# First norm of each layer: scales and biases in the first group's forget-gate buffers, and the scaled centring in two halves

## The chip, the cores and the metric

The kernel runs on one core of one Trainium2 chip. The metric is the device time of one execution in microseconds (us). Timed runs are separate from the profiled execution, which has a time of its own. The engines are PE (TensorE, matrix products), DVE (VectorE), ACT (ScalarE), POOL (GpSimd) and SP (SyncE, which here issues all transfers). Each engine works through its own list of instructions in order, so an instruction that waits holds up all that stand behind it on its engine.

## What is computed

Two layers of a decoder trunk on 512 tokens of width 1024. Each layer projects x once, runs four groups of attention heads (A, forgetting attention; B, latent; C, stick-breaking; D, sliding window), normalises and joins them, projects back and adds; then comes a norm, a gated feed-forward block and a second norm:

```python
y = _group_rmsnorm(mix, mix_g[l]) @ w_o[l]
x = _layernorm(ALPHA * x + y, ln1_g[l], ln1_b[l])
f = (silu(x @ w_gate[l]) * (x @ w_up[l])) @ w_down[l]
x = _layernorm(ALPHA * x + f, ln2_g[l], ln2_b[l])

def _layernorm(x, g, b, eps=1e-5):
    mu = mean(x); var = mean((x - mu) ** 2)
    return (x - mu) * rsqrt(var + eps) * g + b
```

Only group A has a forget gate; its bias enters the scores as one more small matrix product per score block, whose operands (one per head) are the four buffers `augh0` to `augh3`.

## The kernel before

The tokens lie in four tiles (t = 0 to 3) of 128 partitions by 1024 columns, `x_res`. fp32 products are made from a high and a low part of each operand (three passes), so each weight block is loaded as `w_raw`, cast to its high part (ACT or POOL, line 727 or 729) and its low part is the difference (DVE or POOL, line 447). The order on every engine is not written by hand: the program is a set of tasks, and a planner (class `Sched`) with a cost for each operation decides once, when the program is built, which instruction comes next on each engine. A change of one cost or one wait can therefore move instructions around it.

Around the first norm of a layer this happens, in order:

- `out_proj(GA, GB)` multiplies the joined heads of groups A and B by `w_o`. For each tile and each half of the columns PE makes a product in a PSUM bank `ps`, and DVE adds it to `x_res` (line 1746). The add for group B also leaves the row sum in `lnst`.
- `layernorm` of a tile: ACT squares both halves (line 801), DVE makes small 128x1 numbers (lines 808, 813, 830, 839, 844), centres and scales all 1024 columns by g in one instruction (line 856), ACT and DVE make the inverse root (lines 478 to 486), and DVE multiplies by it and adds b in two halves (line 861).
- Each half, when done, is turned by four PE transposes (`ps<-ident,x_res`, line 754), and its high and low parts are written to `xT` by ACT (line 458) and DVE (line 447).
- `up(0, 1)`, the first two blocks of `w_gate` and `w_up`, multiplies `xT`, first for the tokens of tiles 0 and 1 in all four weights, then for tiles 2 and 3. These four weights are loaded into the two `w_raw` buffers, one after the other (the second `w_gate` and the second `w_up` after the first ones are split), and their parts go to `qk` buffers.
- After that `up_pair` makes the other blocks two at a time from seven half-size pieces with sums of the operands ("11", "12", "s2", "s1", "s3", "s4", "22").

g and b of a norm are each loaded as 128 x 1024 numbers, one into the buffer `mixf`, one into `vd`, each of which there is only one. `mixf` holds the joined heads of a group before the norm, last those of group B; so this load has to wait until group B's are read for the last time (line 449, `mix<-mixf`). SP issues its transfers in program order; the load of g and b stands there ahead of the first `w_gate`. The last norm of the kernel works with `hurry`, in which the last tile is centred in halves already.

Of the kernel before, what the change touches and what calls it, by code (L numbers as in the profile page):

```python
# [21 lines left out]
F32 = mybir.dt.float32  # L22
# [3 lines left out]
ALU = mybir.AluOpType  # L26
# [3 lines left out]
P = 128  # L30
S = 512
D = 1024
NT = S // P
# [13 lines left out]
GA, GB, GC, GD = range(4)  # L47
# [18 lines left out]
E_PE, E_ACT, E_DVE, E_POOL, E_SP = range(5)  # L66
# [11 lines left out]
def join(*deps):  # L78

    if any(x is None for x in deps):  # L80
        return None
    return tuple(map(max, zip(*deps))) if len(deps) > 1 else deps[0]


def mark(e, t):
    return NOW[:e] + (t,) + NOW[e + 1:]
# [33 lines left out]
class Sched:  # L120
# [9 lines left out]
    def spawn(self, gen, prio=0, order=None):  # L130
        self.n += 1
        self.step((gen, prio, self.n if order is None else order), None)
# [220 lines left out]
def trunk(ctx: ExitStack, tc: tile.TileContext, d):  # L353
    nc = tc.nc
    ACT, DVE, POOL, PE = nc.scalar, nc.vector, nc.gpsimd, nc.tensor
# [6 lines left out]
    sb = ctx.enter_context(tc.tile_pool(name="sb", bufs=1))  # L362
# [11 lines left out]
    r_vd = Ring(sb, "vd", 1, [P, NT, 2, 2, 64], F32R)  # L374
    r_mix = Ring(sb, "mix", 2, [P, 2, 2, S], F32R)
    r_mixf = Ring(sb, "mixf", 1, [P, 2, S], F32)
# [24 lines left out]
    x = const.tile([P, NT, D], F32, name="x_res")  # L401
# [12 lines left out]
    def dma(out, in_, us=0.0, dep=NOW):  # L414

        e = yield Op(E_SP, 450.0, dep)
        nc.sync.dma_start(out=out, in_=in_)
        sched.dma = max(sched.dma, e[E_SP] + 800.0) + us * 1e3
        return mark(E_SP, sched.dma + 1100.0)
# [22 lines left out]
    f = f32  # L442
# [334 lines left out]
        spawn(task(), LOW)  # L777

    def ln_load(g, b):
        gb, bb = r_mixf.take([P, D], F32), r_vd.take([P, D], F32)  # L780
        e1 = yield from dma(gb.tile, g.partition_broadcast(P), 1.46, gb.dep)
        e2 = yield from dma(bb.tile, b.partition_broadcast(P), 1.46, bb.dep)
        return gb, bb, join(e1, e2)

    def layernorm(t, vecs, st, dep, later, then, hurry=False):

        gb, bb, loaded = vecs
        prio = LOW if hurry and t < NT - 1 else 0  # L790
        e_ = E_POOL if hurry else E_DVE
        small = engines[e_]
# [1 line left out]
        def one(tensors=False):  # L794
            return 130.0 if e_ == E_DVE else 150.0 if tensors else 265.0
# [11 lines left out]
        e = yield Op(e_, one(), dep)  # L807
# [4 lines left out]
        e = yield Op(E_DVE, 130.0, second, prio)  # L812
        DVE.tensor_scalar(out=st[:, 5:6], in0=st[:, 1:2], scalar1=st[:, 0:1], scalar2=-1.0 / D, op0=ALU.add, op1=ALU.mult)
        centred = [x[:, t, :512], x[:, t, 512:]]
        held, early = [], {}
        if hurry and t == NT - 1:

            def centre(e):
                yield lambda: r_temp.ready(2)
                held.extend([r_temp.take(), r_temp.take()])  # L820
                for c in range(2):
                    g = yield Op(E_DVE, 663.0, join(e, loaded, held[c].dep))
                    DVE.scalar_tensor_tensor(out=held[c].tile, in0=centred[c], scalar=st[:, 5:6], in1=gb.tile[:, c * 512:c * 512 + 512],
                                             op0=ALU.add, op1=ALU.mult)
                    centred[c] = held[c].tile
                early["done"] = g

            spawn(centre(e), 0, t - NT)
        b = yield Op(e_, one(), second)
        small.tensor_scalar(out=st[:, 6:7], in0=st[:, 1:2], scalar1=st[:, 0:1], scalar2=1.0 / D, op0=ALU.subtract, op1=ALU.mult)  # L830
        if hurry:
            b = yield Op(e_, one(True), b)
            small.tensor_tensor(out=st[:, 7:8], in0=st[:, 6:7], in1=st[:, 6:7], op=ALU.mult)
        a = yield lambda: squared.get(0)
        b = yield Op(e_, one(hurry), join(a, b))
# [4 lines left out]
        a = yield lambda: squared.get(1)  # L840
# [11 lines left out]
        if hurry and t == NT - 1:  # L852
            e = yield lambda: early.get("done")
        else:
            e = yield Op(E_DVE, 1196.0, join(a, e, loaded), prio)
            DVE.scalar_tensor_tensor(out=x[:, t], in0=x[:, t], scalar=st[:, 5:6], in1=gb.tile, op0=ALU.add, op1=ALU.mult)  # L856
        r = yield lambda: squared.get("r")
        for c in range(2):
            csl = slice(c * 512, (c + 1) * 512)
            e = yield Op(E_DVE, 663.0, join(a, r, e), prio)  # L860
            DVE.scalar_tensor_tensor(out=x[:, t, csl], in0=centred[c], scalar=st[:, 9:10], in1=bb.tile[:, csl], op0=ALU.mult, op1=ALU.add)  # L861
            if c:
                x_dep[t] = e
            then(t, c, e)
# [4 lines left out]
    def layer(l):  # L869
# [5 lines left out]
        at = {}  # L875
# [1189 lines left out]
        def norm(g, b, then):  # L2065
            vecs = []

            def load():
                def task():
                    yield lambda: join(r_mixf.ready(), r_vd.ready()) if g != "ln1_g" or ("mix", GB) in at else None  # L2070
                    vecs.append((yield from ln_load(d[g][l], d[b][l])))

                at["ffn"] = mark(E_PE, sched.free[E_PE])
                spawn(task(), 0, 0)
                return
                yield

            count = Joint(2 * NT, lambda dep: [h.give(dep) for h in vecs[0][:2]])

            def last(t, st, dep, later):  # L2080
                def then_(t, c, e):
                    count.add(e)
                    then(t, c, e)
                spawn(layernorm(t, vecs[0], st, dep, later, then_, g == "ln2_g" and l == DEPTH - 1), 0, t - NT)

            last.loaded = vecs
            return load, last
# [178 lines left out]
```

## Time and profile before

| what | value |
|---|---|
| median of 3 timed runs | 1234.24 us (1234.1 to 1234.76) |
| the profiled execution's own time | 1237.61 us |
| its span in the trace | 1235.8 us |
| PE busy | 1193.6 us, 97% of the span |
| DVE busy | 890.8 us, 72% |
| ACT busy | 673.8 us, 55% |
| POOL busy | 248.2 us, 20% |
| transfers | 110.74 MB, mean 90 GB/s |

PE is busy nearly all the time, so time can be won only where PE waits or runs at its lower clock. The shares are means over stages: in the few stages where PE has gaps another engine is full. A matmul's record ends some time after the next one began, so the distance between starts says more than a single duration.

### The profile page before, as it was taken

To read this page: it belongs to the slowest core of one execution; us is meant where nothing else is said; L and a number is where in the kernel's file an instruction comes from. 1 tells how busy PE (TensorE), PEld (TensorE's weight loads), DVE (VectorE), ACT (ScalarE), POOL (GpSimd) and SP (SyncE) were. 2 spreads that over 40 slices of the span, in tenths; PEclk is the share of its full clock that TensorE was granted. 3 is DMA by queue.
4 is the path that set the end of the run, shared out by engine and by line. 5 is a ranking of instruction groups with operands and counts; after the bars stand their busy time and mean duration, and the time that the engine had idled before them with its cause. 6 is when DMAs were issued, how large, how long until landed. Compare 5 with 4: busy or idle time off the path is not lost.

```text
span 1235.8 us, 20319 instructions
## 1 busy us (share of the span) xinstructions
PE 1193.6 (97%) x7669; PEld 1084.0 (88%) x7669; DVE 890.8 (72%) x1668; ACT 673.8 (55%) x1427; POOL 248.2 (20%) x267
## 2 busy tenths in 40 slices
PE   8999999989999999999999999999899999999996
PEld 7989878769999889998889888787899999899985
DVE  5668668699997557982665786787999956489625
ACT  4749859456655334562357687583555643266421
POOL 3542653400000000000035536643000000000003
PEclk9989999989999999999999999999999999999999
DMA  6312220413332243324233121303223331342341
GB/s 198 87 42 54 68 89 14 119 46 104 110 106 83 86 153 86 103 86 136 85 70 86 42 63 42 103 20 118 86 86 103 103 120 51 120 120 86 103 136 68
DMA packets 111586, 110.74 MB, mean 90 GB/s; under 512 B 9729, under 2 KB 94593, under 8 KB 111489
## 3 DMA queue, kind: packets, MB, share of 16 engines
q1 hardware_dynamic: 111488, 109.45, 29.7%
q8 instruction: 60, 0.98, 0.3%
q14 instruction: 38, 0.30, 0.1%
HBM read 107.34 MB, written 2.10 MB: 89 GB/s over the span
## 4 chain that ended last, share of the span: by engine, by line
PE 82%; DVE 10%; ACT 3%; issue 2%; DMA 1%; POOL 1%; SPq 0%; DVEq 0%; POOLq 0%; ACTq 0%
PE ps L469 79%; PE ps L1560 2%; DVE qk L447 1%; DMA w_raw<-in_w_gate 1%; DVE x_res L1746 1%; DVE xT L447 1%; DVE x_res L861 1%; DVE x_res L856 1%; DVE pt L447 1%; PE ps L754 1%; ACT xT L727 0%; DVE qk L449 0%; DVE temp L1309 0%; DVE augk L1095 0%; DVE mix L449 0%
## 5 line engine op out<-in xcount | busy, mean ns | idle before, releaser
L469 PE MATMUL ps<-xT,w_hi 128*128 128x256 f32 (+1 forms) x1128 | 218.4, 321 | 0.3 <-DVE xT L447 0.3
L469 PEld LDWEIGHTS ps<-xT,w_hi 128*128 128x128 f32 x1128 | 164.5, 193 | 12.5 <-DVE xT L447 0.5
L469 PE MATMUL ps<-w_hi,qk 128*128 128x512 f32 (+1 forms) x560 | 171.0, 387 | 0.0
L469 PE MATMUL ps<-xT,w_lo 128*128 128x256 f32 (+1 forms) x888 | 167.2, 306 | 0.0
L727 ACT CAST w_hi<-w_raw 128x1024 fp32r<-128x1024 f32 (+2 forms) x86 | 87.8, 1022 | 108.8 <-PE ps L469 87.2
L447 POOL TENSOR_TENSOR w_lo<-w_raw,w_hi 128x1024 fp32r<-128x1024 f32 (+4 forms) x66 | 120.8, 1839 | 108.1 <-ACT w_hi L727 81.7
L447 DVE TENSOR_TENSOR w_lo<-w_raw,w_hi 128x1024 fp32r<-128x1024 f32 x47 | 57.6, 1226 | 112.3 <-ACT w_hi L727 112.2
L469 PEld LDWEIGHTS ps<-xT,w_lo 128*128 128x128 f32 x888 | 124.5, 192 | 7.6
L469 PEld LDWEIGHTS ps<-w_hi,qk 128*128 128x128 f32 x560 | 104.2, 188 | 20.8
L469 PE MATMUL ps<-w_hi,mix 128*128 128x512 f32 x352 | 110.9, 396 | 3.5 <-DVE xT L447 3.5
L469 PE MATMUL ps<-w_lo,qk 128*128 128x512 f32 (+1 forms) x280 | 108.1, 386 | 0.0
L1914 ACT COPY temp<-ps 128x256 f32<-128x256 f32 x120 | 44.7, 372 | 83.3 <-PE ps L469 82.8
L775 POOL TENSOR_SCALAR x_res<-x_res 128x1024 f32<-128x1024 f32 x8 | 8.9, 1120 | 376.3 <-PE ps L754 376.3
L664 ACT CAST w_hi<-temp 128x512 fp32r<-128x512 f32 x78 | 48.4, 620 | 64.2 <-DVE temp L607 35.1
L469 PEld LDWEIGHTS ps<-w_hi,mix 128*128 128x128 f32 x352 | 65.1, 190 | 17.0 <-issue 4.3
L664 ACT CAST w_lo<-temp 128x512 fp32r<-128x512 f32 x82 | 50.7, 620 | 46.6 <-DVE temp L607 32.0
L447 DVE TENSOR_TENSOR w_hi<-temp,w_hi 128x512 fp32r<-128x512 f32 x78 | 53.3, 688 | 30.5 <-ACT w_hi L664 30.3
L469 PE MATMUL ps<-xT,qk 128*128 128x256 f32 x528 | 70.2, 294 | 1.0 <-DVE lnst L484 0.7
L469 PE MATMUL ps<-w_lo,mix 128*128 128x512 f32 x176 | 69.2, 393 | 0.8 <-DVE pt L447 0.4
L469 PEld LDWEIGHTS ps<-xT,qk 128*128 128x128 f32 x528 | 67.9, 201 | 1.9 <-DVE qk L447 1.4
L469 PE MATMUL ps<-w_hi,xT 128*128 128x388 f32 (+1 forms) x256 | 68.8, 350 | 0.4 <-DVE qk L449 0.4
L808 POOL TENSOR_SCALAR lnst<-lnst 128x1 f32<-128x1 f32 x4 | 0.8, 190 | 330.2 <-DVE x_res L2006 330.2
(236 smaller groups left out, 2710.3 us busy)
## 6 DMA issues: line engine op xcount, KB each, us to landing
w_raw<-in_w_down SPq DMA_DIRECT2D x44, 512.0 KB, 3.7
w_raw<-in_w_in SPq DMA_DIRECT2D x26, 512.0 KB, 3.7
w_raw<-in_w_gate SPq DMA_DIRECT2D x24, 512.0 KB, 3.7
w_raw<-in_w_up SPq DMA_DIRECT2D x24, 512.0 KB, 3.7
w_raw<-in_w_o SPq DMA_DIRECT2D x16, 512.0 KB, 3.7
mixf<-in_w_up SPq DMA_DIRECT2D x10, 512.0 KB, 3.7
vd<-in_w_up SPq DMA_DIRECT2D x10, 512.0 KB, 3.7
mixf<-in_w_gate SPq DMA_DIRECT2D x10, 512.0 KB, 3.8
```

The costliest lines, as they stand in the source:

```text
L447: eng.tensor_tensor(out=lo, in0=src, in1=f(hi), op=ALU.subtract)
L469: PE.matmul(out, lhsT=lhsT, rhs=rhs, start=start, stop=stop, skip_group_check=True)
L664: ACT.copy(out=self.part[0], in_=src)
L727: ACT.copy(out=out, in_=in_ if psum is None else psum)
L754: PE.transpose(out=u.tile[:, k * P:(k + 1) * P], in_=x[:, t, kk * P:(kk + 1) * P], identity=ident)
L775: POOL.tensor_scalar(out=x[:, t], in0=x[:, t], scalar1=ALPHA, scalar2=0.0, op0=ALU.mult, op1=ALU.add)
L808: small.tensor_scalar(out=st[:, 2:3], in0=st[:, 0:1], scalar1=-1.0 / (32 * 512), scalar2=0.0, op0=ALU.mult, op1=ALU.add)
L856: DVE.scalar_tensor_tensor(out=x[:, t], in0=x[:, t], scalar=st[:, 5:6], in1=gb.tile, op0=ALU.add, op1=ALU.mult)
L861: DVE.scalar_tensor_tensor(out=x[:, t, csl], in0=centred[c], scalar=st[:, 9:10], in1=bb.tile[:, csl], op0=ALU.mult, op1=ALU.add)
L1560: PE.transpose(out=u.tile[:, k * P:(k + 1) * P], in_=p.tile[:, k * P:(k + 1) * P], identity=ident)
L1746: DVE.scalar_tensor_tensor(out=x[:, t, csl], in0=ps.tile, scalar=rs[:, t:t + 1], in1=x[:, t, csl], op0=ALU.mult, op1=ALU.add, accum_out=st ...
L1914: ACT.copy(out=dst, in_=src)
```

## The change

The load of the first norm's g and b no longer goes to `mixf` and `vd`. It goes, as four 128 x 512 pieces, into the four `augh` buffers, and may start as soon as group A's joined heads are finished (`("mix", GA)`), where before it waited for group B's (`("mix", GB)`). The second norm still loads into `mixf` and `vd`. For all norms the centring is done in two instructions of 512 columns instead of one of 1024.

```diff
     def ln_load(g, b):
+
         gb, bb = r_mixf.take([P, D], F32), r_vd.take([P, D], F32)
         e1 = yield from dma(gb.tile, g.partition_broadcast(P), 1.46, gb.dep)
         e2 = yield from dma(bb.tile, b.partition_broadcast(P), 1.46, bb.dep)
-        return gb, bb, join(e1, e2)
+        return [[v.tile[:, :512], v.tile[:, 512:]] for v in (gb, bb)] + [join(e1, e2), (gb, bb)]
+
+    def ln_load_early(g, b, dep):
+
+        v, loaded = [], []
+        for i, a in enumerate((g, b)):
+            v.append([sb.tile([P, 512], F32, name=f"lnv{h}", tag=f"augh{h}", bufs=1) for h in (2 * i, 2 * i + 1)])
+            for c in range(2):
+                loaded.append((yield from dma(v[i][c], a[c * 512:c * 512 + 512].partition_broadcast(P), 0.73, dep)))
+        return v + [join(*loaded), ()]
...
-            e = yield Op(E_DVE, 1196.0, join(a, e, loaded), prio)
-            DVE.scalar_tensor_tensor(out=x[:, t], in0=x[:, t], scalar=st[:, 5:6], in1=gb.tile, op0=ALU.add, op1=ALU.mult)
+            for c in range(2):
+                e = yield Op(E_DVE, 663.0, join(a, e, loaded), prio)
+                DVE.scalar_tensor_tensor(out=centred[c], in0=centred[c], scalar=st[:, 5:6], in1=gb[c], op0=ALU.add, op1=ALU.mult)
...
                 def task():
-                    yield lambda: join(r_mixf.ready(), r_vd.ready()) if g != "ln1_g" or ("mix", GB) in at else None
-                    vecs.append((yield from ln_load(d[g][l], d[b][l])))
+                    if g == "ln1_g":
+                        dep = yield lambda: at.get(("mix", GA))
+                        vecs.append((yield from ln_load_early(d[g][l], d[b][l], dep)))
+                    else:
+                        yield lambda: join(r_mixf.ready(), r_vd.ready())
+                        vecs.append((yield from ln_load(d[g][l], d[b][l])))
```

The new line numbers of the two halves of the centring are 867, of the final scaling 872, of the add of a product to `x_res` 1757, and of the small numbers 818, 823, 840, 849, 854 (before: 856, 861, 1746, and 808, 813, 830, 839, 844). SP's list stays as it was but for the load itself (four transfers for two, still between the last `w_o` and the first `w_gate`) and for `mixf` and `vd`, which change places in later loads. The planner also moves other instructions, in both layers in the same way. Three places, in layer 0:

DVE at the first norm, from the add for tile 0 on. `qk<-w_raw` is the low part of the first `w_gate`; `ps_2704` and `ps_2713` are the products for the second half of tile 0 and the first of tile 1. Before:

```order
L1746 SCALAR_TENSOR_TENSOR x_res,lnst<-ps_2695,rsg,x_res 128x512
L808 TENSOR_SCALAR lnst<-lnst 128x1
L1746 SCALAR_TENSOR_TENSOR x_res,lnst<-ps_2704,rsg,x_res 128x512
L447 TENSOR_TENSOR qk_2686<-w_raw_2656,qk_2685 128x1024
L813 TENSOR_SCALAR lnst<-lnst 128x1
L830 TENSOR_SCALAR lnst<-lnst 128x1
L1746 SCALAR_TENSOR_TENSOR x_res,lnst<-ps_2713,rsg,x_res 128x512
L839 TENSOR_SCALAR lnst<-lnst 128x1
L856 SCALAR_TENSOR_TENSOR x_res<-x_res,lnst,mixf_2661 128x1024
```

Now (`ps_2708` and `ps_2718` are the same two products):

```order
L1757 SCALAR_TENSOR_TENSOR x_res,lnst<-ps_2699,rsg,x_res 128x512
L447 TENSOR_TENSOR qk_2690<-w_raw_2664,qk_2689 128x1024
L818 TENSOR_SCALAR lnst<-lnst 128x1
L1757 SCALAR_TENSOR_TENSOR x_res,lnst<-ps_2708,rsg,x_res 128x512
L1757 SCALAR_TENSOR_TENSOR x_res,lnst<-ps_2718,rsg,x_res 128x512
L823 TENSOR_SCALAR lnst<-lnst 128x1
L840 TENSOR_SCALAR lnst<-lnst 128x1
L818 TENSOR_SCALAR lnst<-lnst 128x1
L849 TENSOR_SCALAR lnst<-lnst 128x1
L867 SCALAR_TENSOR_TENSOR x_res<-x_res,lnst,lnv_2623 128x512
L854 TENSOR_SCALAR lnst<-lnst 128x1
L867 SCALAR_TENSOR_TENSOR x_res<-x_res,lnst,lnv_2624 128x512
```

The low part of the weight now stands ahead of the second add of tile 0 and of the first small number; the centring is two instructions and reads `lnv`.

PE at the end of the output projection: the last products for group A in tiles 2 and 3 (`v`, `w_hi` with `mix`) and the transposes of tile 0. Before:

```order
L469 MATMUL ps_2760<-w_lo_2526,mix_2372 128x512
L469 MATMUL ps_2774<-v_2485,mix_2372 128x512 x3
L469 MATMUL ps_2774<-w_hi_2525,mix_2372 128x512 x2
L469 MATMUL ps_2774<-w_lo_2526,mix_2372 128x512
L754 MATMUL ps_2793<-ident,x_res 128x128 x4
L469 MATMUL ps_2790<-w_hi_2623,mix_2625 128x512 x2
```

Now:

```order
L469 MATMUL ps_2769<-w_lo_2526,mix_2372 128x512
L754 MATMUL ps_2789<-ident,x_res 128x128 x4
L469 MATMUL ps_2784<-v_2485,mix_2372 128x512 x3
L469 MATMUL ps_2784<-w_hi_2525,mix_2372 128x512 x2
L469 MATMUL ps_2784<-w_lo_2526,mix_2372 128x512
L754 MATMUL ps_2792<-ident,x_res 128x128 x4
```

The first transposes stand one product (six matmuls) earlier.

ACT at the first pair of up blocks: `temp<-ps` copies a result out of PSUM, `qk<-temp` is the high part of a finished hidden block, and the `w_hi<-temp` that comes last before (`w_hi_3015`) and second now (`w_hi_3030`) is the high part of piece "s2". Before:

```order
L664 CAST w_hi_3016<-temp_3017 128x512
L1866 CAST qk_3187<-temp_3189 128x512
L1914 COPY temp_3192<-ps_3190 128x256
L664 CAST w_hi_3015<-temp_3208 128x512
L664 CAST w_hi_3206<-w_raw_2994 128x512
```

Now:

```order
L664 CAST w_hi_3031<-temp_3032 128x512
L1866 ACTIVATE temp_3198<-ps_2987 128x512
L664 CAST w_hi_3030<-temp_3190 128x512
L664 CAST w_lo_3044<-temp_3205 128x512
L1925 COPY temp_3202<-ps_3200 128x256
L1877 CAST qk_3197<-temp_3199 128x512
L664 CAST w_hi_3219<-w_raw_3008 128x512
```

The cast of "s2" moved from behind the copy out of PSUM, which needs PE's first piece, to ahead of it. On DVE its low part likewise moved from behind the add that uses that copy (line 1919 before, 1930 now) to ahead of it.

## Rows read from the trace of the kernel before

**Rows 1.** The page: the span, and the chain that ended last, by engine.

```profile
span 1235.8 us, 20319 instructions
PE 82%; DVE 10%; ACT 3%; issue 2%; DMA 1%; POOL 1%; SPq 0%; DVEq 0%; POOLq 0%; ACTq 0%
```

**Rows 2.** Waits of PE over the whole span: who waited for whom, us in total, times, longest.

```profile
PE ps L754 <- DVE x_res L861: 12.5, 9, 2.9
...
PE ps L469 <- DVE w_hi L447: 1.9, 2, 0.9
```

**Rows 3.** Timeline of SP in layer 0: start, duration of the issue, transfer (the last three `w_o` are merged in one row).

```profile
218.93 8.82 SPq L417 DMA_DIRECT2D w_raw<-in_w_o  x3
237.84 0.33 SPq L417 DMA_DIRECT2D mixf<-in_ln_g  x1
...
238.73 0.38 SPq L417 DMA_DIRECT2D w_raw<-in_w_gate  x1
...
248.36 0.37 SPq L417 DMA_DIRECT2D w_raw<-in_w_gate  x1
```

**Rows 4.** Timeline of ACT and POOL in layer 0: start, duration, line, out<-in; in brackets the idle time before and what ended it.

```profile
246.03 1.05 ACT L727 CAST qk<-w_raw 128x1024 fp32r<-128x1024 f32 x1 [9.70 <-DMA w_raw<-in_w_gate]
...
234.84 2.42 POOL L447 TENSOR_TENSOR w_lo<-w_raw,w_hi 128x1024 fp32r<-128x1024 f32 x1 [7.46 <-ACT w_hi L727]
...
252.02 1.04 POOL L729 TENSOR_SCALAR qk<-w_raw 128x1024 fp32r<-128x1024 f32 x1 [2.10 <-DMA w_raw<-in_w_gate]
```

**Rows 5.** Timeline of DVE in layer 0.

```profile
241.76 0.75 DVE L1746 SCALAR_TENSOR_TENSOR x_res<-ps,rsg,x_res 128x512 f32<-128x512 f32 x1 [0.61 <-PE ps L469]
...
243.12 0.75 DVE L1746 SCALAR_TENSOR_TENSOR x_res<-ps,rsg,x_res 128x512 f32<-128x512 f32 x1 [0.41 <-PE ps L469]
...
247.11 1.23 DVE L447 TENSOR_TENSOR qk<-w_raw,qk 128x1024 fp32r<-128x1024 f32 x1 [3.23 <-ACT qk L727]
...
249.35 1.64 DVE L856 SCALAR_TENSOR_TENSOR x_res<-x_res,lnst,mixf 128x1024 f32<-128x1024 f32 x1
...
274.26 1.22 DVE L447 TENSOR_TENSOR qk<-w_raw,qk 128x1024 fp32r<-128x1024 f32 x1
```

**Rows 6.** Timeline of PE in layer 0.

```profile
249.72 0.84 PE L469 MATMUL ps<-v,mix 128*128 128x512 f32 x3
...
254.10 1.11 PE L754 MATMUL ps<-ident,x_res 128*128 128x128 f32 x4 [2.86 <-DVE x_res L861]
...
269.08 0.63 PE L754 MATMUL ps<-ident,x_res 128*128 128x128 f32 x4 [2.10 <-DVE x_res L861]
...
279.05 11.16 PE L469 MATMUL ps<-xT,qk 128*128 128x256 f32 x91
```

**Rows 7.** Stretches: from:to, length, then busy time (and instructions) of PE, PEld, DVE, ACT, POOL, the granted clock of PE as a share of full speed, DMA share, GB/s. From the low part of the first `w_gate` to that of the second, layers 0 and 1, and four microseconds of layer 0.

```profile
247.11:275.48 28.37, 22.36 (x117) 18.43 (x115) 27.18 (x65) 14.75 (x37) 2.09 (x2) 0.88 0.13 39
857.12:884.50 27.38, 21.74 (x120) 18.24 (x118) 26.78 (x65) 14.80 (x37) 2.72 (x2) 0.94 0.13 39
...
253.00:257.00 4.00, 2.90 (x9) 2.50 (x10) 3.87 (x10) 1.16 (x5) 0.07 (x1) 0.57 0.00 0
```

**Rows 8.** Timeline of layer 1: POOL, DVE and PE rows that answer to those of layer 0.

```profile
845.64 2.42 POOL L447 TENSOR_TENSOR w_lo<-w_raw,w_hi 128x1024 fp32r<-128x1024 f32 x1 [7.62 <-ACT w_hi L727]
...
852.56 0.75 DVE L1746 SCALAR_TENSOR_TENSOR x_res<-ps,rsg,x_res 128x512 f32<-128x512 f32 x1 [0.61 <-PE ps L469]
...
857.12 1.22 DVE L447 TENSOR_TENSOR qk<-w_raw,qk 128x1024 fp32r<-128x1024 f32 x1 [2.44 <-ACT qk L727]
...
888.06 5.16 PE L469 MATMUL ps<-xT,qk 128*128 128x256 f32 x41
```

**Rows 9.** The chain that ended last in layer 0, in order of time: start, length, engine, tile and line. One centring and one final scaling, as steps of the chain (to the start of the next step).

```profile
263.54 1.20 DVE x_res L856
...
269.06 0.66 DVE x_res L861
```

**Rows 10.** Lines 856 and 861 over the whole span: count, shortest, median and longest duration in ns, first and last start.

```profile
L856 DVE SCALAR_TENSOR_TENSOR x_res<-x_res,lnst,mixf x15: 1272/1276/1640, 249.4 to 1224.2; 128x1024 f32<-128x1024 f32 x15
...
L861 DVE SCALAR_TENSOR_TENSOR x_res<-x_res,lnst,vd x30: 736/748/870, 253.3 to 1232.1; 128x512 f32<-128x512 f32 x30
```

**Rows 11.** Timeline of ACT, DVE and PE at the first pair of up blocks, layer 0.

```profile
295.17 0.38 ACT L1914 COPY temp<-ps 128x256 f32<-128x256 f32 x1
295.44 0.62 ACT L664 CAST w_hi<-temp 128x512 fp32r<-128x512 f32 x1
...
296.68 0.43 DVE L1919 TENSOR_TENSOR ps<-ps,temp 128x256 f32<-128x256 f32 x1 [0.81 <-ACT w_hi L664]
...
297.76 2.90 PE L469 MATMUL ps<-v,w_hi 128*128 128x256 f32 x22 [0.95 <-DVE w_hi L447]
```

**Rows 12.** Timeline of DVE and PE at the second norm of layer 0, third tile.

```profile
619.56 0.75 DVE L861 SCALAR_TENSOR_TENSOR x_res<-x_res,lnst,vd 128x512 f32<-128x512 f32 x1
...
620.36 0.66 PE L754 MATMUL ps<-ident,x_res 128*128 128x128 f32 x4 [1.70 <-DVE x_res L861]
```

**Rows 13.** The chain at the end of the kernel: DVE's scalings of two tiles, between which POOL makes the inverse root.

```profile
1217.30 0.75 DVE x_res L861
...
1221.98 0.75 DVE x_res L861
```

**Rows 14.** The `augh` buffers over the whole span: PE's readings, count, durations in ns, first and last start.

```profile
L469 PE MATMUL ps<-augk,augh x32: 279/362/478, 139.4 to 802.1; 128*128 128x128 f32 x8, 128*128 128x256 f32 x8, 128*128 128x384 f32 x8, 128*128 128x512 f32 x8
```

More of the change, by code (lines that the diff above doesn't have):

```diff
@@ L782, in ln_load @@
         e2 = yield from dma(bb.tile, b.partition_broadcast(P), 1.46, bb.dep)
-        return gb, bb, join(e1, e2)
+        return [[v.tile[:, :512], v.tile[:, 512:]] for v in (gb, bb)] + [join(e1, e2), (gb, bb)]
[6 more added lines that the diff above has]
+        return v + [join(*loaded), ()]
     def layernorm(t, vecs, st, dep, later, then, hurry=False):
-        gb, bb, loaded = vecs
+        gb, bb, loaded, _ = vecs
         prio = LOW if hurry and t < NT - 1 else 0
@@ L822, in centre @@
                     g = yield Op(E_DVE, 663.0, join(e, loaded, held[c].dep))
-                    DVE.scalar_tensor_tensor(out=held[c].tile, in0=centred[c], scalar=st[:, 5:6], in1=gb.tile[:, c * 512:c * 512 + 512],
+                    DVE.scalar_tensor_tensor(out=held[c].tile, in0=centred[c], scalar=st[:, 5:6], in1=gb[c],
                                              op0=ALU.add, op1=ALU.mult)
@@ L860, in layernorm @@
             e = yield Op(E_DVE, 663.0, join(a, r, e), prio)
-            DVE.scalar_tensor_tensor(out=x[:, t, csl], in0=centred[c], scalar=st[:, 9:10], in1=bb.tile[:, csl], op0=ALU.mult, op1=ALU.add)
+            DVE.scalar_tensor_tensor(out=x[:, t, csl], in0=centred[c], scalar=st[:, 9:10], in1=bb[c], op0=ALU.mult, op1=ALU.add)
             if c:
@@ L2076, in load @@
                 yield
-            count = Joint(2 * NT, lambda dep: [h.give(dep) for h in vecs[0][:2]])
+            count = Joint(2 * NT, lambda dep: [h.give(dep) for h in vecs[0][3]])
             def last(t, st, dep, later):
```

## Prediction

> **What bounds the kernel now.** I read the chain that ended last first: PE holds 82% of it [rows 1], so time is won only where PE stands still or runs at its lower clock. PE's waits come next: the largest is the transposes waiting for the scaled x, 12.5 us in nine waits, and a smaller one is for a weight's low part, 1.9 us in two [rows 2]. The timelines then say where these lie. In layer 0 PE stands 2.86 us before tile 0's transposes and 2.10 before tile 2's [rows 6]. While PE stands still DVE is full: in the stretch from the first `w_gate`'s low part to the second's DVE works 27.18 of 28.37 us, PE 22.36; in layer 1 it is 26.78 of 27.38 against 21.74 [rows 7]. So the bound of this stage is DVE's list, and the question is when it can start and how long it is.
>
> It starts late because of a transfer. DVE's low part of the first `w_gate` begins at 247.11 after 3.23 us of idling for ACT's cast [rows 5], and ACT's cast begins at 246.03 after 9.70 us for the transfer [rows 4]. That transfer was issued at 238.73, behind the load of g and b at 237.84 [rows 3]; so it took 7.3 us. The third load of the stage, also a `w_gate` but with nothing ahead of it, was issued at 248.36 and in use at 252.02: 3.66 us [rows 3, 4].
>
> **Part 1: the load moves out of the way.** SP's last `w_o` is issued before 227.75 (218.93 + 8.82) [rows 3]; the load may start when group A is finished, so after its last product with the `augh` buffers (in layer 1 that is at 802.1, over 40 us ahead of the norm) [rows 8, 14]. The four new transfers can therefore go out from about 228, some 15 us before the first centring reads them. What then holds the first `w_gate` is its `w_raw` buffer alone. POOL's split gives it back at 234.84 + 2.42 = 237.26 [rows 4], so it goes out 1.5 us earlier and travels alone: 237.26 + 3.66 = 240.9, and ACT's cast of 1.05 ends at 242.0. DVE is free at 241.76 + 0.75 = 242.5, after the add that PE's product releases [rows 5]. DVE comes later than the cast, so DVE's low part starts at 242.5 instead of 247.11: **4.6 us earlier**. Layer 1: buffer free at 845.64 + 2.42 = 848.06, cast done by 848.06 + 3.66 + 1.05 = 852.8, DVE free at 852.56 + 0.75 = 853.3 against 857.12 now [rows 8]: **3.8 us earlier**. The margin of the transfer is 0.5 us; each microsecond by which it lands later than that is lost one for one.
>
> **Part 2: what stands on DVE in between.** The stretch to the second `w_gate`'s low part now holds also the second add of tile 0 and its small number, which stood ahead of the low part (0.75 [rows 5], with some 0.1 for the small one: 0.86), two small numbers of tile 3 that moved ahead (0.2), and four centrings in halves. Two halves cost 2 x 0.66 against 1.20 as steps of the chain [rows 9], 0.12 to 0.14 each, or 2 x 0.748 - 1.276 = 0.22 by medians [rows 10]. I take 0.14, the steps being what an engine that is never idle pays; 0.22 is the upper end. Four make 0.56 (0.88). The sum is 1.6 us (1.9).
>
> The stretch gets 27.18 + 1.6 = 28.8 in layer 0, less up to 0.36, since the first centring took 1.64 instead of 1.28 beside a POOL cast [rows 5] that is now ACT's; with 0.2 of issue gaps I take 28.6. Layer 1: 26.78 + 1.6 + 0.2 = 28.6. DVE is then through at 242.5 + 28.6 = 271.1 instead of 275.48, and at 853.3 + 28.6 = 881.9 instead of 884.50: 4.4 and 2.6 us earlier. No wait of DVE for PE is in this: a product comes every 1.36 us ahead of 249.72 (243.12 and 241.76 are the starts of two adds that waited for such), and DVE's list reaches each add after its product.
>
> Can PE follow? Its transposes of tile 0 now stand where PE arrives at 249.72 [rows 6]. The rows ahead of the first scaled half on DVE, from 242.5 on, are the low part, three adds behind it, two half centrings and twelve small numbers: 1.14 + 3 x 0.74 + 2 x 0.67 + some 1.7, then 0.67 for the half itself: 249.6. PE finds it ready within a few tenths, so the wait of 2.86 goes, and its like in layer 1 and with it the low clock of 253 to 257 (0.57 granted, that is mostly at 1.2 of 2.4 GHz) [rows 7]. From 249.72 to 271.1 there are 21.4 us for what PE did before from 249.72 to 275.48, of which it was busy 22.36 - 2.61 (247.11 to 249.72) = 19.7. PE keeps 1.7 us of slack, and DVE stays the bound: smaller waits before the transposes of tile 2 and before the low parts remain.
>
> **Part 3: the way out of the stage.** Before, PE began the fourth block 279.05 - 275.48 = 3.57 us after the second `w_gate`'s low part [rows 5, 6]. Now tile 3's scaling stands right behind that low part and its transposes earlier on PE, so PE waits one half (0.73), then has two groups of transposes (0.35 each) and 21 matmuls of 0.123 (11.16 over 91): 4.0. That loses 0.5 in each layer. Left of the stage: 3.9 and 2.1.
>
> **Part 4: piece "s2".** In each layer PE stands 0.95 us in the first pair because "s2"'s cast stands behind a copy that needs PE's first piece (295.17, then 295.44), and its low part behind the add at 296.68 [rows 11]. In the new lists both stand ahead of these, and DVE has them done when PE starts the first piece. Both waits (1.9 in all [rows 2]) go. The engines ahead of them are early too, since DVE reaches this place some 4 us earlier, as PE does.
>
> **Part 5: the second norms pay.** In layer 0's second norm the third tile's scaling (619.56) releases PE after a wait of 1.70 [rows 12]; three centrings in halves stand ahead, and ACT's steps to the inverse root come a little later: 0.4 to 0.7, I take **0.5 lost**. At the end of the kernel DVE scales a tile every 4.68 us (1217.30 to 1221.98 [rows 13]) and idles for POOL in between; a centring of 1.28 that grows by 0.2 fits into that. No loss.
>
> The rule that speaks against halves is in the Trainium skill, "VectorE: DVE Perf Modes", section on the TRN2 errata: an operation that reads SBUF pays a fixed extra per instruction, with about 150 cycles measured. At that page's 0.96 GHz this is an estimate of 0.16 us for each added instruction, between my two ends of 0.14 and 0.22; by it the sum above would be 0.2 us worse.
>
> **Sum.** 3.9 + 2.1 + 1.9 - 0.5 = 7.4 us. The profiled execution took 1237.61, so it would take 1230.2; the median is 3.4 lower than that execution, and 1234.24 - 7.4 = **1226.9**. What a measurement tells from no change is about 0.2%, 2.5 us.
>
> **The rivals.**
> *Low clock (gain about 4).* PE still stops briefly several times between 255 and 271, and behind stops of 2 us the trace shows stretches at the lower clock (0.57) [rows 7]. There its work takes twice as long: if the two up blocks of 24 matmuls before the second `w_gate` (2 x 24 x 0.123 = 5.9 us) run at 1.2 GHz all through, they cost 5.9 more, against a slack of 1.7 and against some 2 of low clock that the busy sum contains already. That takes about 2 us from each layer: 1231.0. For it: the stops do not vanish. Against it: they are shorter than now.
> *All of PE's waits go (gain about 12).* 12.5 + 1.9 would give some 1221. Against it: DVE's list fills the stage and got longer.
> *No earlier weight (no change).* If the transfer lands no earlier, DVE starts at 247.11 and 857.12 as now and needs 28.6 us instead of 28.37 and 27.38; with part 3 that loses 0.7 and 1.7, the second norm 0.5, and part 4 wins 1.9: 1235.2.
> *Halves on the path (slower).* The skill's rule, as a mechanism of this kernel: fifteen centrings [rows 10] each lose 0.22 on a path that DVE ends, 3.3 us, with the start of the stage unchanged and part 4's wait only moved to the next piece: 1237.5. It decides if the first `w_gate` lands later than about 245, that is, if it wins under 1 us. Against it: the load that stood ahead of it is away.
>
> **Chances.** Forecast 0.62 (1224.5 to 1229); low clock 0.22; all waits 0.03; no change 0.08; slower 0.05. Faster by over 0.2%: the forecast, all waits and nearly all of the low clock case, 0.86; within 0.2%: 0.09; slower: 0.05. The range from 1224 to 1231.5 takes in the forecast and most of the low clock case.
>
> **What will show it.** ACT's cast of the first `w_gate` at about 241 (layer 1: 852), DVE's low part at 242.5 and 853.3; no wait over 0.5 us before tile 0's transposes; DVE full from 242.5 to about 271; PE's fourth block at about 275 and 886; no wait at "s2"; the third tile's wait in layer 0's second norm at about 2.2 instead of 1.70. I am wrong if the cast comes later than 243, or if DVE idles in the stage, or if PE's granted clock over the stage falls well below 0.88.

## The result, and the profile after

Five timed runs of the changed kernel take 1229.13 us (1225.38 to 1230.08) beside 1234.76 of the kernel before, a ratio of 0.9944 (95% interval 0.9931 to 0.9957): 5.3 to 8.5 us faster. A second series of it (e11 below) gave 0.9931 (0.9917 to 0.9945). The profiled execution takes 1229.42, with a span of 1227.6.

The page of the profile after, span and chain (answers to [rows 1]; the DMA share of the chain is gone), and the first of PE's waits (answers to [rows 2]; line 872 was 861, 1757 was 1746):

```profile
span 1227.6 us, 20339 instructions
PE 83%; DVE 10%; ACT 3%; issue 3%; POOL 1%; DVEq 0%; POOLq 0%; ACTq 0%
...
PE ps L754 <- DVE x_res L872: 6.1, 5, 2.1
...
PE ps L469 <- DVE qk L447: 3.2, 4, 1.2
...
PE ps L469 <- DVE x_res L1757: 1.3, 2, 0.7
```

The wait for the scaled x fell from 12.5 to 6.1 us; the one for s2 (`w_hi` L447, 1.9) is gone; the wait for low parts of weights (`qk` L447) grew from 0.2 to 3.2.

Layer 0 of the profile after: SP, ACT, DVE and PE (answers to [rows 3 to 6]):

```profile
229.37 0.90 SPq L417 DMA_DIRECT2D lnv<-in_ln_g  x2
230.32 0.90 SPq L417 DMA_DIRECT2D lnv<-in_ln_b  x2
238.52 0.38 SPq L417 DMA_DIRECT2D w_raw<-in_w_gate  x1
...
236.66 2.38 DVE L449 SCALAR_TENSOR_TENSOR mix<-mixf,mg,mix 128x512 fp32r<-128x512 f32 x1 [0.47 <-ACT mix L460]
242.17 1.05 ACT L727 CAST qk<-w_raw 128x1024 fp32r<-128x1024 f32 x1 [4.61 <-DMA w_raw<-in_w_gate]
246.82 1.05 ACT L727 CAST qk<-w_raw 128x1024 fp32r<-128x1024 f32 x1 [0.26 <-DMA w_raw<-in_w_up]
...
243.66 1.22 DVE L447 TENSOR_TENSOR qk<-w_raw,qk 128x1024 fp32r<-128x1024 f32 x1
...
250.95 0.60 PE L754 MATMUL ps<-ident,x_res 128*128 128x128 f32 x4
...
264.95 0.63 PE L754 MATMUL ps<-ident,x_res 128*128 128x128 f32 x4 [1.28 <-DVE x_res L872]
...
271.89 0.73 PE L469 MATMUL ps<-xT,qk 128*128 128x256 f32 x4 [1.19 <-DVE qk L447]
...
292.91 3.04 PE L469 MATMUL ps<-v,w_hi 128*128 128x256 f32 x24
```

The load is out at 229.37, nine microseconds ahead of `w_gate`, which now travels alone (238.52 to the cast at 242.17: 3.65). DVE goes into the low part at 243.66 without idling, PE into tile 0's transposes at 250.95 and into s2 at 292.91 without a wait.

Stretches from the start of the first `w_gate`'s low part to the end of that of the second, layers 0 and 1, and four microseconds of layer 0 (answers to [rows 7], same columns):

```profile
243.66:271.83 28.17, 23.96 (x137) 20.08 (x135) 27.93 (x76) 15.06 (x37) 1.05 (x1) 1.00 0.19 56
847.63:875.83 28.20, 23.98 (x137) 20.10 (x136) 27.93 (x76) 15.57 (x38) 1.05 (x1) 1.00 0.19 55
...
253.00:257.00 4.00, 4.00 (x24) 3.17 (x22) 4.00 (x11) 0.96 (x2) 0.00 (x0) 1.00 0.00 0
```

DVE is full, as before, and PE's granted clock is 1.00 over the stage (0.88 and 0.94 before).

**Where the time lies in every run.** The start of a stage moves by microseconds between executions (last section), so all runs are compared from fixed marks of the trace. The first mark is the start of group B's last product on DVE (`mix<-mixf`, line 449); the second column gives how long behind it the low part of the first `w_gate` starts. S: from that mark to PE's first product behind s2 (`pt,w_lo`), which holds the stage and s2; N: from there to layer 1's first `ps<-xT,w_hi` on PE, which holds layer 0's second norm; T: from DVE's last instruction to the end of the span. The last but one column adds S, N, T and the stretch from layer 1's s2 to DVE's last instruction (323.2 to 324.0 in all runs) and gives the difference from before; the last is the timed ratio. The ratios leave out three single executions that took far longer (1459.19 of the kernel before, 4121.66 of e5, 2350.59 of e10).

| run | low part of `w_gate`, layers 0, 1 | S, layers 0, 1 | N | T | sum against before | ratio (95%) |
|---|---|---|---|---|---|---|
| before | 11.68, 10.90 | 65.07, 63.28 | 340.83 | 2.91 | | |
| after | 7.00, 7.02 | 59.13, 59.17 | 341.56 | 4.65 | -7.8 | 0.9944 (0.9931 to 0.9957) |
| e11, the same again | 7.01, 7.01 | 59.24, 59.15 | 341.03 | 4.66 | -8.2 | 0.9931 (0.9917 to 0.9945) |
| e1 halves, load late | 11.09, 11.18 | 63.42, 63.69 | 341.05 | 3.05 | -1.1 | 1.0008 (0.9998 to 1.0019) |
| e2 lists of e1, load early | 8.40, 8.37 | 60.45, 61.73 | 341.43 | 3.80 | -4.9 | 0.9956 (0.9944 to 0.9968) |
| e6 lists of after, load late | 12.82, 12.32 | 66.75, 65.51 | 341.43 | 3.19 | +4.6 | 1.0043 (1.0031 to 1.0055) |
| e5 lists of after, load behind `w_gate` | 7.01, 7.16 | 60.99, 60.77 | 341.43 | 4.37 | -4.8 | 0.9970 (0.9959 to 0.9981) |
| e7 lists of before, load behind `w_gate` | 8.37, 8.37 | 62.13, 61.45 | 340.44 | 2.92 | -5.2 | 0.9969 (0.9957 to 0.9981) |
| e3 planned so, whole centring | 7.55, 7.36 | 66.09, 64.41 | 340.69 | 2.87 | +1.8 | 1.0020 (1.0008 to 1.0032) |
| e9 early load, whole centring | 7.01, 7.00 | 64.09, 64.03 | 340.28 | 2.99 | -0.8 | 0.9995 (0.9987 to 1.0004) |
| e10 the same, other order | 7.02, 7.02 | 59.07, 59.07 | 341.06 | 2.93 | -9.3 | 0.9929 (0.9910 to 0.9948) |
| e4 after, second norm whole | 7.02, 7.01 | 59.18, 59.15 | 340.30 | 3.48 | -10.1 | 0.9936 (0.9916 to 0.9956) |
| e8 e4, two low parts on POOL | 7.01, 7.01 | 60.15, 61.89 | 340.46 | 3.50 | -6.1 | 0.9966 (0.9952 to 0.9979) |

So the change won 5.94 and 4.11 us in S, lost 0.2 to 0.7 in N and 1.75 at the end. The stretch from the end of N to layer 1's group B is in no sum: it took 203.3 to 203.4 in the profiles whose granted clock between 685 and 705 us is 1.00 (after and e11 among them), and 204.9 to 205.0 in those where it is 0.91 (before among them).

### The profile page after: what moved, and what is told of

Its sections match the earlier page's. It is cut to its first block, busy times and chain, and to the rows that moved or that the text cites. A ratio compares the mean times of both kernels' runs of the same rounds, so it can differ in the third digit from the quotient of the medians.

```text
span 1227.6 us, 20339 instructions
## 1 busy us (share of the span) xinstructions
PE 1188.4 (97%) x7669; PEld 1079.9 (88%) x7669; DVE 891.4 (73%) x1683; ACT 675.2 (55%) x1429; POOL 245.3 (20%) x265
## 4 chain that ended last, share of the span: by engine, by line
PE 83%; DVE 10%; ACT 3%; issue 3%; POOL 1%; DVEq 0%; POOLq 0%; ACTq 0%
PE ps L469 80%; PE ps L1571 2%; DVE x_res L1757 1%; DVE qk L447 1%; DVE xT L447 1%; DVE pt L447 1%; DVE x_res L872 1%; PE ps L754 1%; ACT xT L727 0%; ACT temp L1459 0%; DVE qk L449 0%; DVE temp L1320 0%; DVE augk L1106 0%; ACT kh L940 0%; PE ps L1711 0%
## 5 line engine op out<-in xcount | busy, mean ns | idle before, releaser
L447 POOL TENSOR_TENSOR w_lo<-w_raw,w_hi 128x1024 fp32r<-128x1024 f32 (+4 forms) x66 | 120.8, 1839 | 109.4 <-ACT w_hi L727 90.5
L447 DVE TENSOR_TENSOR w_lo<-w_raw,w_hi 128x1024 fp32r<-128x1024 f32 x47 | 57.6, 1225 | 112.2 <-ACT w_hi L727 112.1
L447 DVE TENSOR_TENSOR w_hi<-temp,w_hi 128x512 fp32r<-128x512 f32 x78 | 53.2, 686 | 30.7 <-ACT w_hi L664 30.5
```

The source lines that it names most:

```text
L447: eng.tensor_tensor(out=lo, in0=src, in1=f(hi), op=ALU.subtract)
```

## The experiments

**Transfer or halves: e1 and e2.** e1 is the changed kernel with the load of before:

```diff
-                    if g == "ln1_g":
-                        dep = yield lambda: at.get(("mix", GA))
-                        vecs.append((yield from ln_load_early(d[g][l], d[b][l], dep)))
...
+                    yield lambda: join(r_mixf.ready(), r_vd.ready()) if g != "ln1_g" or ("mix", GB) in at else None
...
```

> The changed kernel with its load put back: g and b of the first norm go to mixf and vd again and wait for group B, so they stand ahead of the first w_gate as before; the centring stays in halves, and the lists around piece s2 are the new ones. If the early load is what wins (theory): ACT's cast of the first w_gate waits for its transfer until about 246 and 856 again, DVE's low part starts at about 247 and 857, the stage is 0.5 to 1 us longer than before in each layer (four more instructions of 0.14, the way out), the second norm of layer 0 loses 0.9 and the two waits at s2 stay gone (2.4 won): 1233.5 to 1236.5. If the halves win by themselves, since PE gets a first half sooner (rival): 1229 to 1231, and no wait over 1 us before tile 0's transposes.

e2 changes one name in the changed kernel:

```diff
-                        dep = yield lambda: at.get(("mix", GA))
+                        dep = yield lambda: at.get(("mix", GB))
```

> The changed kernel with one word changed: its four pieces still go to the augh buffers but may start only when group B's heads are joined, so they go out just ahead of the first w_gate. If the time of the load is what wins, and not the buffers (theory): as with the load put back, cast of the first w_gate at 246 to 247 and 856 to 857, 1233.5 to 1237. If the place of the data wins (rival: mixf and vd free sooner for later loads): 1229 to 1231.

Layer 0 of e1, then of e2: the load, the cast of the first `w_gate`, its low part.

```profile
239.19 0.33 SPq L417 DMA_DIRECT2D mixf<-in_ln_g  x1
246.78 1.05 ACT L727 CAST qk<-w_raw 128x1024 fp32r<-128x1024 f32 x1 [9.09 <-DMA w_raw<-in_w_gate]
247.87 1.23 DVE L447 TENSOR_TENSOR qk<-w_raw,qk 128x1024 fp32r<-128x1024 f32 x1 [2.60 <-ACT qk L727]
```

```profile
225.51 0.90 SPq L417 DMA_DIRECT2D lnv<-in_ln_g  x2
238.29 1.05 ACT L727 CAST qk<-w_raw 128x1024 fp32r<-128x1024 f32 x1 [4.50 <-DMA w_raw<-in_w_gate]
241.28 1.22 DVE L447 TENSOR_TENSOR qk<-w_raw,qk 128x1024 fp32r<-128x1024 f32 x1
```

e1 gave 1.0008: the halves and the new place of s2 win nothing together; the rival falls. e2's time (1230.98) lies in the range of its rival, but shows nothing for it, because its edit did not do what its expectation says: the wait for `("mix", GB)` exists only in the plan. On the chip the `augh` buffers are free, and the load went out at 225.51, right behind the last `w_o`. That makes it the cleaner experiment: e1 and e2 have the same instructions in the same order on DVE, ACT, PE and POOL; on SP they differ in the load (and in which of `mixf` and `vd` later loads take first). With the load early the same lists are 0.52% faster (1.0008 to 0.9956, 6.4 us).

**The other half of the square: e6.** e1 and e2 are one pair of lists with the load late and early; the changed kernel is the other lists with it early, and e6 those with it late. To hold the load back for real, DVE writes one column of the first piece behind group B's last product. The four transfers are planned as in the changed kernel, so that the planner's lists stay the same, but kept in `held_back` and issued only there by `let_go()`:

```diff
                 at["mix", g] = join(*out)
+                if g == GB:
...
+                    DVE.memset(held_back[0][0][:, :1], 0.0)
+                    let_go()
```

> The changed kernel with its lists as they were, and a real wait for the load: DVE sets one column of the first piece right behind group B's last product (128x1, one instruction more in each layer), and the load of that piece waits for it, the other three behind it. Theory: the w_gate again lands at 245 to 247, and since its low part now stands ahead of the second add and the first small number of tile 0, DVE holds these back too: worse than the lists of before with the same lateness (1237.2) by 0.5 to 2: 1237.5 to 1239.5. Rival, the new lists win by themselves whatever the transfer does: 1230 to 1234.

DVE and PE in layer 0 of e6, then a stretch of it:

```profile
245.78 1.22 DVE L460 TENSOR_TENSOR qk<-w_raw,qk 128x1024 fp32r<-128x1024 f32 x1 [5.72 <-ACT qk L742]
...
252.68 1.12 PE L769 MATMUL ps<-ident,x_res 128*128 128x128 f32 x4 [5.23 <-DVE x_res L887]
```

```profile
253.00:257.00 4.00, 4.00 (x15) 3.32 (x13) 4.00 (x9) 0.79 (x2) 0.00 (x0) 0.50 0.00 0
```

1.0043, slower than before by some 5 us and about 1 more than expected. The new lists need the early weight: DVE idles 5.72 with the second add queued behind it, PE 5.23, and behind that PE works at 0.50, that is at 1.2 GHz. Part of the loss is a transfer later than in e1: four issues stand ahead of `w_gate` here and two there, and its low part starts 1.73 and 1.14 us later behind group B's product.

The low-clock rival of the prediction is thus a real mechanism, and a shorter stop had it too. In e4 (below), whose stage has the lists and the load of the changed kernel, PE's granted clock fell in layer 0 behind a stop of 1.29:

```profile
266.00:270.00 4.00, 3.30 (x16) 3.26 (x16) 4.00 (x10) 2.20 (x6) 0.00 (x0) 0.57 0.17 50
```

There it cost nothing: PE's later waits are shorter, and S is 59.18, as without it.

**Only the order of two transfers: e7 and e5.** Both hold the load back in the same way, until the first `w_gate` is issued, and change nothing else on any engine; e7 starts from the kernel before, e5 from the changed one. In the loading of a weight:

```diff
             self.loaded = e
+            if any(c is self for c in first_up):
...
+                let_go()
```

> The kernel before, whose instructions stand on DVE, ACT, PE and POOL exactly as they were; on SP alone the load of g and b stands behind the first w_gate. Theory: w_gate's cast at about 242 and 853, its low part at 243.9 and 854.6 (behind the second add, where the old list has it): 3.2 and 2.5 us earlier, 1230 to 1231.5. Rival, the lists of before don't suit the early weight and PE waits elsewhere, as where the planner knew of the order: 1233 to 1237.

> The changed kernel, whose instructions stand on DVE, ACT, PE and POOL exactly as they were; on SP alone the four transfers of g and b stand behind the first w_gate instead of ahead of it. In the run with the order of before changed the w_gate took 4.6 us beside them instead of 3.65, and b landed 6.7 us after its issue. If it only matters that w_gate doesn't stand behind the load (theory): w_gate's cast 0.5 to 1 us later than in the changed kernel, g and b there by 246 to 247 against a first centring at 247: 0.5 to 1 us lost in each layer, 1230 to 1231.5 beside 1229.3 of the changed kernel and 1236.2 of before. If the early load is needed as such (rival): DVE waits for g at the first centring, 1233 or more.

ACT, DVE and PE in layer 0 of e5:

```profile
243.11 1.05 ACT L743 CAST qk<-w_raw 128x1024 fp32r<-128x1024 f32 x1 [5.00 <-DMA w_raw<-in_w_gate]
249.38 1.05 ACT L743 CAST qk<-w_raw 128x1024 fp32r<-128x1024 f32 x1 [2.27 <-DMA w_raw<-in_w_up]
...
251.51 0.27 DVE L495 TENSOR_SCALAR lnst<-lnst 128x1 f32<-128x1 f32 x1 [1.75 <-ACT lnst L493]
...
253.11 0.66 PE L770 MATMUL ps<-ident,x_res 128*128 128x128 f32 x4 [1.46 <-DVE x_res L888]
```

e7 gave 0.9969 (1231.5 us): swapping two transfers on SP, without new buffers or halves, wins 3.8 us of the 6.9. e5 gave 0.9970, worse than expected. Its first `w_gate` is in time; what is late is the next weight: `w_up`, issued into the rest of the load, is cast at 249.38 after a wait of 2.27, which is 12.18 us behind group B's product instead of 10.16, and behind that cast on ACT stand the steps to tile 0's inverse root, for which DVE idles 1.75 and PE 1.46. So the early load is worth something beyond the order: 1.6 to 1.9 us of S in each layer.

**What the halves are worth: e3, e9, e10 and e4.** e3 tells the planner to put the load of before behind the first `w_gate`; e9 has the early load without halves (two `augh` buffers of twice the width); e10 is e9 with one cost changed; e4 is the changed kernel with the instruction of 1024 columns back in the second norms. The first three in this order:

```diff
-yield lambda: join(r_mixf.ready(), r_vd.ready()) if g != "ln1_g" or ("mix", GB) in at else None
+yield lambda: join(r_mixf.ready(), r_vd.ready()) if g != "ln1_g" or (("mix", GB) in at and at["gate_first"].loaded) else None
...
-            heads = [sb.tile([P, S], F32R, name=f"augh{h}", tag=f"augh{h}", bufs=1) for h in range(4)]
+            wide = [sb.tile([P, 2 * S], F32R, name=f"augh{h}", tag=f"augh{h}", bufs=1) for h in range(2)]
...
-            e = yield Op(E_DVE, 1196.0, join(a, e, loaded), prio)
+            e = yield Op(E_DVE, 1080.0, join(a, e, loaded), prio)
```

> The kernel before with one more condition: its load of g and b (to mixf and vd, as before) goes out behind the first w_gate instead of ahead of it; centring in one instruction. If the order of the two transfers is the whole matter (theory): cast of the first w_gate at 241 to 242.5 and 851 to 853 (4.6 and 3.8 us earlier), g and b land by 247, before the first centring wants them at 248 to 249; the gain of the changed kernel in the stage comes (7.6 by its trace), and four times 0.14 in each layer and the second norm's 0.9 aren't paid: 1223.5 to 1227. Rival: g and b come too late, and DVE waits 1 to 4 us for them at the first centring: 1228 to 1234.

> Early load without halves: the four augh buffers become two of twice the width (so that 1024 numbers of g lie together), g and b go there as early as in the changed kernel, and every centring is one instruction again, with the planner's own order (cost 1196). In that order the low parts of the first w_up and the second w_gate stand behind tile 3's centring, as where w_gate was planned first, and there PE waited 3.5 us for one of them in each layer. If what the halves are worth is the better place that the planner gives to these low parts (theory): 1234 to 1238 although the weight is early. If halves only cost (rival): 1227 to 1229.

> The same with one number changed, the planner's cost of that centring, 1080 instead of 1196, by which it puts the low part of the first w_up ahead of tile 3's centring, as in the changed kernel, and s2 ahead too. Theory: the changed kernel's stage without 4 x 0.14 us in each layer, and the second norm's 0.9 not paid: 1226.5 to 1228.5, PE's wait of 3.5 gone. Rival, the first half tile that comes sooner is worth as much as the halves cost: 1229 to 1231.

> The changed kernel, but the second norm of both layers centres all 1024 columns in one instruction again (the first norm's stay in halves). If the halves cost the second norm of layer 0 what the traces say (PE comes out of it 0.86 us later, 0.45 of that before the third tile's transposes): 0.9 faster than the changed kernel, 1227.5 to 1229, the wait before the third tile back at 1.7. If the 0.86 belongs to something else (rival): as the changed kernel, 1229 to 1230.

PE and DVE in layer 0 of e9 (e3 has the same wait of PE, 3.53):

```profile
270.78 4.42 PE L469 MATMUL ps<-xT,qk 128*128 128x256 f32 x19 [3.54 <-DVE lnst L484]
...
269.51 1.22 DVE L447 TENSOR_TENSOR qk<-w_raw,qk 128x1024 fp32r<-128x1024 f32 x1
```

The stretch of e10 that answers to the first of the changed kernel, but ends just behind the start of the second `w_gate`'s low part (269.82; it ends at 271.04), and the gap in it on DVE:

```profile
242.80:270.00 27.20, 24.09 (x137) 20.14 (x136) 26.45 (x69) 14.97 (x37) 1.05 (x1) 1.00 0.20 58
```

```profile
269.63 0.27 DVE L482 TENSOR_SCALAR lnst<-lnst 128x1 f32<-128x1 f32 x1 [0.39 <-ACT lnst L480]
```

e3 lost (1.0020, beyond both its lines) and e9 won nothing (0.9995, as expected), although their first weights were early and in e3 g and b were there in time (first centring at 243.64 without a wait). With a cost of 1196 the planner sets the low part of the first `w_up` behind tile 3's centring, and PE stands 3.5 us for it in each layer. (The row of PE names `lnst` L484, a small number that DVE makes between this low part and the next; PE starts 0.05 us behind the low part's end.) Behind that stop PE works at the lower clock, as in e6:

```profile
270.78:275.00 4.22, 4.22 (x19) 4.22 (x20) 2.68 (x5) 0.00 (x0) 0.00 (x0) 0.50 0.75 239
```

In e3's layer 0 the second weight is late besides, as in e5: ACT waits 1.80 for `w_up`, PE 1.50 before tile 0. e10 changes one number, by which the planner sets that low part ahead and moves some other instructions with it, and gets all: 0.9929, beside 0.9931 of the changed kernel on the same chip. So in the stage halves and whole centring are worth the same (S 59.07 against 59.13 to 59.24), and what the halves did was to bring about a good order.

e4 gave 0.9936, not to be told from the changed kernel, so the 0.9 of its expectation is not shown by time. Its trace has the wait before the third tile of layer 0's second norm back at 1.70, against 2.15 in the profile after (e4, then after):

```profile
615.94 0.66 PE L754 MATMUL ps<-ident,x_res 128*128 128x128 f32 x4 [1.70 <-DVE x_res L875]
```

```profile
615.97 0.66 PE L754 MATMUL ps<-ident,x_res 128*128 128x128 f32 x4 [2.15 <-DVE x_res L872]
```

Over all runs N is 341.03 to 341.56 with halves in the second norm and 340.28 to 341.06 without: 0.7 between the means.

**More for the same bottleneck: e8.** e4 with two of the low parts on POOL, which is idle in the stage.

```diff
-rings=(r_qk, r_qk) if len(js) > 1 else None, low=E_DVE if len(js) > 1 else None,
+rings=(r_qk, r_qk) if len(js) > 1 else None, low=(E_POOL if (n, j) in (("w_up", 0), ("w_gate", 1)) else E_DVE) if len(js) > 1 else None,
```

> The changed kernel with the second norm's centring in one instruction, and the low parts of the first w_up and the second w_gate made by POOL instead of DVE. If DVE's list bounds the stage (theory): it is 2.4 us shorter in each layer, less what DVE loses beside POOL's 4.8 us (a centring beside a POOL cast took 1.64 instead of 1.28), PE's wait of 1.19 for the second w_gate's low part goes: 1 to 2.4 us won in each layer, 1224.5 to 1227.5. Rival, POOL slows DVE by as much as it takes from it: 1229 to 1231.

POOL and DVE in layer 0 of e8:

```profile
246.69 2.70 POOL L447 TENSOR_TENSOR qk<-w_raw,qk 128x1024 fp32r<-128x1024 f32 x1 [5.83 <-ACT qk L727]
249.71 2.46 POOL L447 TENSOR_TENSOR qk<-w_raw,qk 128x1024 fp32r<-128x1024 f32 x1 [0.33 <-ACT qk L727]
...
247.03 0.75 DVE L1760 SCALAR_TENSOR_TENSOR x_res<-ps,rsg,x_res 128x512 f32<-128x512 f32 x1
...
249.98 2.75 DVE L875 SCALAR_TENSOR_TENSOR x_res<-x_res,lnst,lnv 128x512 f32<-128x512 f32 x1
```

0.9966: the rival, and more. One scaling of 0.74 took 2.75 and ended 0.6 behind POOL's second low part, beside which it had begun. The add that reads PSUM (247.03) took its usual 0.75 in the middle of POOL's first. The waits at s2 are back too (2.3 us in two). The Trainium skill, "SBUF — State Buffer", section "SBUF: two separate sides", says that a VectorE instruction with two SBUF inputs and a GpSimd instruction that reads SBUF hold the port pair they share each for its whole length, the later one standing still. The trace agrees with that rule: 2.75 for 0.74. The expectation's 1.64 for 1.28, read from one centring beside a cast, was far too little.

**The change once more: e11.**

> The changed kernel once more, on the same chip as the two others: 1228 to 1230.5, and a second profile of it. If the 8.2 us between the first two profiles were partly the clock ahead of the stage and the end of the program (theory), the stage (7.00 us from group B's product to the low part of w_gate, 28.2 to that of the second w_gate) repeats to 0.1, while the time ahead of the stage moves by up to 4 us.

0.9931, and the stage repeats: 7.01 us to the low part in both layers, S within 0.11 of the first profile, and the stretch of layer 0, same columns as above:

```profile
240.00:268.20 28.20, 23.99 (x137) 20.07 (x135) 27.95 (x76) 15.05 (x37) 1.05 (x1) 1.00 0.19 56
```

## Why the prediction was right

The forecast was faster, 1226.9 in 1224.0 to 1231.5, by a sum of 7.4. The two series have 6.9 and 8.5 by their ratios, the marks of the trace 7.8 and 8.2. The time of 1229.13 lies just above the likeliest case's own range (1224.5 to 1229) and inside the whole one. Step by step:

- **Part 1 held, in mechanism and size.** Low part 4.68 and 3.88 us earlier against group B's product (forecast 4.6 and 3.8), transfer 3.65 (3.66). e1 with e2 shows that the transfer is the cause. What the step left out is the second weight: e5 shows that a load moved only behind `w_gate` makes `w_up` late.
- **Part 2: right that DVE's list bounds, slightly off in size.** The stretch is 28.17 and 28.20 (28.6 forecast), so DVE is through 4.9 and 3.1 us earlier (4.4 and 2.6). The waits named as going (2.86, and with it the low clock) went; the ones named as remaining remained (1.28 and 0.71 before tile 2, 1.19 before the second `w_gate`'s low part). The price of the halves is there on DVE, about 0.44 for four instead of 0.56 (27.93 busy with them; without, in e10, 26.45 and 1.04 for the rest of the last low part). But without them DVE idles more: 0.75 us not busy, 0.24 with them. The stretch is 28.24 there: on the path the price is nothing.
- **Part 3 was too dear.** The way out cost 0.5 by forecast. From DVE's end of the second low part to PE's first product of the first pair ("11") the stages lost 0.15. The stages won 4.73 and 2.90 in all (58.10 to 53.37, 56.31 to 53.41; 3.9 and 2.1 forecast).
- **Part 4 held, and was too small.** The waits of 0.95 went, and each was worth 1.2 (5.94 - 4.73, 4.11 - 2.90). e1 has the new place of s2 without the early load, and e3 and e9, which have no halves, lose the waits too: any of these changes of the plan moves s2, and it does not take the early weight on the chip.
- **Part 5: layer 0's second norm as forecast, the end not.** The third tile's wait is 2.15 (2.2 forecast), the price 0.7 over all runs (0.5). DVE's last rows show no loss at the end, as written; but the span ends 4.65 us behind DVE instead of 2.91. This 1.75 is the term that was missing, and it is about what the other terms were short of. SP's waits for the last stores, over the last 8 us before and after, hold it:

```profile
SPq L2254 <- DMA out_x<-x_res: 1.1, 2, 0.6
```

```profile
SPq L2269 <- DMA out_x<-x_res: 2.9, 2, 1.8
```

- **The rivals.** "No change" and "halves on the path" fell with the cast at 242.17. "All of PE's waits go" fell with the 6.1 that remain (its own sum, 12.5 + 1.9, gives 1219.8 and not 1221). "Low clock" did not occur in the two profiles of the changed kernel (1.00 over the stage); e6 and e9 have it behind their long stops, and where the same stage had it for a few microseconds (e4) it cost nothing.

The sum was right within a microsecond with terms that were 1.6, 0.5, -0.2 and -1.75 off. The mechanism was right and its parts were not exact; that the sum came out so close is luck, since the loss at the end, which it did not have, made up for gains that it had too small.

What the prediction lacked altogether is how much the early weight's worth depends on the order around it. In the square of lists and transfer (e1, e2, e6, after) the early load is worth 6.4 us with the one lists and 12 with the other, of which nearly 3 would be e6's later `w_gate` if its 1.73 and 1.14 are lost one for one; the new lists with the late load lose 5.3 against before, and there too the low part is 1.14 and 1.42 later than before. With the lists of before an early `w_gate` is worth 3.8 (e7), with the planner's own for whole centring nothing (e9). I took the lists from the plan and the times from the trace, which served here.

## What to carry to other kernels

Look at what stands ahead of a late transfer in the issuing engine's list: a load that is needed later, or could have gone long before, costs whatever stands behind it, and two lines that swap them may win half of what new buffers do. Judge such an edit together with the instruction order it brings about, since the gain of the early data, the place of its consumers and the next transfer in the row decide together. To tell them apart hold all lists fixed and move one transfer, and check in the trace that an edit of a planner's wait has really moved it.

## What the runs showed that I had not expected

- **The end of the program.** Behind the last store the changed kernel's transfers show one more small movement, in both its profiles in the same place, and the span ends there. The last 8 us of the profile before and of the one after, GB/s in 40 slices:

```profile
GB/s 0 0 256 399 379 277 0 0 0 0 0 0 0 0 0 0 0 0 0 0 0 0 0 328 379 358 369 410 369 389 389 369 410 164 41 0 0 0 0 0
```

```profile
GB/s 0 0 0 0 0 0 0 0 0 0 0 0 0 0 215 379 369 389 369 379 399 369 379 399 266 21 41 0 0 0 0 0 0 0 0 0 0 0 41 0
```

  The instruction queue's count for these 8 us is one packet before and two after. T is 2.87 to 4.66 over the runs, 4.37 to 4.66 in the two kernels with exactly the lists of the changed one (after, e5), but 3.19 in e6, which has two instructions more on DVE. The movement alone does not cost the time: e10 has one just ahead of its end too, and its T is 2.93. What goes with T is SP's wait for the last stores in these 8 us: 1.1 before, 1.4 in e10, 1.7 in e4 and e6, 2.0 in e2, 2.9 in after, e11 and e5. Why the stores land later stays open.
- **The clock far ahead of the stage.** Between 150 and 165 us the granted clock was 0.89 before, 0.77 after and 1.00 in e11, and group B's product began at 235.43, 236.66 and 232.99: up to 3.7 us between two executions of the same program, as much as half of the change's gain. Columns as above, after and e11:

```profile
150.00:165.00 15.00, 15.00 (x80) 13.69 (x79) 7.74 (x19) 9.47 (x22) 8.66 (x8) 0.77 0.11 36
```

```profile
150.00:165.00 15.00, 15.00 (x97) 13.54 (x96) 8.02 (x19) 10.30 (x25) 11.01 (x13) 1.00 0.11 36
```

  PE is busy all through in both, and in both it makes 32 products of one column each there (`ps<-ones,temp`, from 150.42 to 154.71 in after); in after the clock fell at 153.05, in e11 it did not. What decides between the two stays open.
